# Folding the time steps of a chunked state-space scan into its decays' exponentials

## The chip, the cores and the metric

The kernel runs on one core of a Trainium2 chip. The core has a matrix engine (PE; its weight loads are shown apart as PEld), a vector engine (DVE), a scalar engine (ACT), GpSimd (POOL) and queues that issue transfers (SP's, ACT's and POOL's). Each engine works through its own instructions in the order in which they stand in the program and waits on semaphores for the others. The metric is the device time of one execution in microseconds. Three executions of the kernel before took 1017.43 to 1017.98 us, with a median of 1017.71.

## What is computed

One block of a hybrid network on 512 tokens of width 1024: an input projection, a convolution branch, a state-space branch (the "scan"), gates that mix the two, and a feed-forward part. The change lies in the scan. It has 32 heads of width 64 in 8 groups of 4; the part of the reference that matters, with `dt` the time steps after a softplus, is

```python
a_dt = dt * a                      # a = -exp(a_log)
a_cs = cumsum(a_dt)                # within a chunk
xdt = x * dt[..., None]
decay_in = exp(where(causal, a_cs[l] - a_cs[s], -inf))
y_diag = einsum("cls,rcls,csrp->clrp", C @ B.T, decay_in, xdt)
decay_to_end = exp(a_cs[-1] - a_cs)
chunk_states = einsum("cln,rcl,clrp->crpn", B, decay_to_end, xdt)
y = y_diag + y_off + x * d_skip
```

`y_off` carries the states from chunk to chunk. Afterwards y is gated by silu(z), normalised by group and projected.

## The kernel before

The scan is worked in 4 chunks of 128 tokens. For a group g, four steps are written as functions. `make_L(g)` fetches the running sums of the group's 4 heads to all partitions through a GpSimd transfer, masks them and forms the tile L by 16 Exp activations on ACT with the bias `nacs` (L496), the negated sums of the other token. `s1(g)` transposes the group's x from channel rows to token rows on PE (tiles pxT, two of 128x512 in PSUM, L667), multiplies each out of PSUM by the time steps (xdt, L670) and by D (y, L671) on DVE, multiplies xdt by the decay to the chunk's end (xdec, L675), transposes B (pBT), multiplies C and B (pcb) and multiplies L by that product (L686, 128x2048). `s2(g)` makes the chunk states (pSa, pSb from xdec and BT, L697), carries them on (prev, L698 to L701) and makes the diagonal part (yd from L and xdt, L709). `s3(g)` adds up y (L717, L734), multiplies by silu(z) and normalises; `s4(g)` transposes y (pyT, L761) and splits it into a high part and a rest (yh on ACT, yl on DVE) for the output projection.

Everything of one group runs beside the large projections of the next: `proj_x(g+1)`, then s1(g), `proj_bc(g+1,"B")` (tile pB), s2(g), `proj_bc(g+1,"C")` (pC), s3(g), and for odd g the gate projections pz (`proj_zz`). A projection is 24 matmuls of 128x512: three products (L246, L248, L252) of high parts (whi, hhi) and rests (wlo, hlo) for each of 8 blocks of 128. Each weight strip is cast to whi on ACT (L202); its rest wlo is made on DVE (L209) or by a GpSimd transfer onto a negated copy (L206, L207). After a projection `conv4` applies four taps: one on ACT out of PSUM (L599), three on DVE (L601), and a Silu on ACT (L605). DVE also works off the 31 taps of the other branch's convolution (tiles a, L514) wherever there is room.

The order on each engine is set by a scheduler that places the recorded instructions by their dependencies and its own estimates of their durations. `by_table` adds an edge that keeps the activations it is given (the Exps, the Silus) in the order of the program, so that the activation tables change seldom. PSUM tiles outside the projections take turns in three banks (`aux_tile`), so a tile can be written only after the tile three turns earlier was read. Before all that, `time_steps` and `running_sums` work out dt (tile dtt), the sums (acs), their exponentials (eacs, dec) and nacs for all heads at once, in tiles of 128x128.

Of the kernel before, what the change touches and what calls it, by code (L numbers as in the profile page):

```python
# [18 lines left out]
P = 128  # L19
# [145 lines left out]
def b3(ap, n):  # L165

    return ap.unsqueeze(len(ap.shape)).to_broadcast(list(ap.shape) + [n])
# [3 lines left out]
def block_kernel(ctx: ExitStack, tc: tile.TileContext, x, xT, x0, prm, hp, gp, wf, w, out):  # L171
# [149 lines left out]
    def flat(a):  # L321
        return a.rearrange("p a b -> p (a b)")
# [135 lines left out]
    def running_sums():  # L458
        pcs = aux_tile("pcs")
        pe.matmul(pcs[:, :CH], tri, flat(ta), start=True, stop=True)  # L460
        act.copy(flat(acs), pcs[:, :CH])
        pend = aux_tile("pend")
        pe.matmul(pend[:, :CH], ones, flat(ta), start=True, stop=True)
        act.activation(flat(cd), pend[:, :CH], AF.Exp)
        act.activation(flat(eacs), flat(acs), AF.Exp)
        dve.tensor_tensor(out=flat(tb), in0=pend[:, :CH], in1=flat(acs), op=ALU.subtract)
        act.activation(flat(dec), flat(tb), AF.Exp)
# [188 lines left out]
    def s1(g):  # L656
        s = st[g]
        hs = slice(HG * g, HG * (g + 1))
        xdt = ssd.tile([P, NT, HG, HD], F32, tag="xdt", name=f"xdt{g}")
        y = ssd.tile([P, NT, HG, HD], F32, tag="y", bufs=2, name=f"y{g}")  # L660
        xdec = ssd.tile([P, NT - 1, HG, HD], F32, tag="xdec", name=f"xdec{g}")
        for c2 in range(2):
            ps = aux_tile(f"pxT{g}_{c2}")
            for c in range(2):
                tok = slice((2 * c2 + c) * P, (2 * c2 + c + 1) * P)
                for e in range(2):
                    pe.transpose(ps[:, c * GW + e * P : c * GW + (e + 1) * P], s[f"x{e}"][:, tok], ident)  # L667
            cs = slice(2 * c2, 2 * c2 + 2)
            pv = ps.rearrange("p (c h d) -> p c h d", c=2, h=HG)
            dve.tensor_tensor(out=xdt[:, cs], in0=pv, in1=b3(dtt[:, cs, hs], HD), op=ALU.mult)  # L670
            dve.tensor_tensor(  # L671
                out=y[:, cs], in0=pv,
                in1=b3(hp_t[:, 2:3, hs].to_broadcast([P, 2, HG]), HD), op=ALU.mult,
            )
        dve.tensor_tensor(out=xdec, in0=xdt[:, : NT - 1], in1=b3(dec[:, : NT - 1, hs], HD), op=ALU.mult)  # L675
# [10 lines left out]
        dve.tensor_tensor(out=L, in0=L, in1=ps.unsqueeze(1).to_broadcast([P, HG, T]), op=ALU.mult)  # L686
        s.update(xdt=xdt, y=y, xdec=xdec, BT=BT)

    def s2(g):
        s = st[g]  # L690
        hs = slice(HG * g, HG * (g + 1))
        prev = ssd.tile([P, NT - 1, HG, HD], F32, tag="prev", name=f"prev{g}")
        tmp = ssd.tile([P, HG, HD], F32, tag="ptmp", bufs=2, name=f"ptmp{g}")
        pa, pb = aux_tile(f"pSa{g}"), aux_tile(f"pSb{g}")
        pS = [pa[:, :GW], pa[:, GW:], pb[:, :GW]]
        for c in range(NT - 1):
            pe.matmul(pS[c], s["BT"][:, c, :], s["xdec"][:, c].rearrange("p h d -> p (h d)"), start=True, stop=True)  # L697
        act.copy(prev[:, 0].rearrange("p h d -> p (h d)"), pS[0])  # L698
        for c in range(1, NT - 1):
            dve.tensor_tensor(out=tmp, in0=prev[:, c - 1], in1=b3(cd[:, c, hs], HD), op=ALU.mult)  # L700
            dve.tensor_tensor(  # L701
                out=prev[:, c], in0=pS[c].rearrange("p (h d) -> p h d", h=HG), in1=tmp, op=ALU.add
            )
        yd = [yd_tile(n, f"yd{g}_{n}").rearrange("p (c h d) -> p c h d", c=2, h=HG) for n in range(2)]
        for c in range(NT):
            for h in range(HG):
                for i in range(0, P, HD):
                    half = slice(i, i + HD)
                    pe.matmul(yd[c // 2][half, c % 2, h, :], s["L"][:, h, c, half], s["xdt"][:, c, h, :], start=True, stop=True)  # L709
        s.update(prev=prev, yd=yd)  # L710

    def s3(g):
# [1090 lines left out]
```

## Time and profile before

| | |
|---|---|
| three executions, median (lowest to highest) | 1017.71 us (1017.43 to 1017.98) |
| span of the profiled execution, first to last instruction | 1016.0 us |
| median less span | 1.7 us |
| instructions in the profiled execution | 15943 |
| busiest engine but PE | DVE, 847.9 us (83% of the span) |
| GpSimd busy | 106.7 us (11%) |
| granted PE clock, mean over the span | 0.998 of full speed |

The profiled execution's own time is not listed apart from its span; the row "median less span" is what lies around the span, by the three timed executions. The scan with its projections runs from about 110 us to 520 us of the span. A row of the timeline reads: start in us, duration in us, engine, line, operation, output and inputs, shape, and in brackets how long the engine sat idle before it and what ended that. Successive matmuls overlap in the record, so a matmul's place is read from the start of the next one.

### The profile page before, as it was taken

To read this page: it belongs to the slowest core of one execution; us is meant where nothing else is said; L and a number is where in the kernel's file an instruction comes from. 1 tells how busy PE (TensorE), PEld (TensorE's weight loads), DVE (VectorE), ACT (ScalarE), POOL (GpSimd) and SP (SyncE) were. 2 spreads that over 40 slices of the span, in tenths; PEclk is the share of its full clock that TensorE was granted. 3 is DMA by queue.
4 is the path that set the end of the run, shared out by engine and by line. 5 is a ranking of instruction groups with operands and counts; after the bars stand their busy time and mean duration, and the time that the engine had idled before them with its cause. 6 is when DMAs were issued, how large, how long until landed. Compare 5 with 4: busy or idle time off the path is not lost.

```text
span 1016.0 us, 15943 instructions
## 1 busy us (share of the span) xinstructions
PE 1007.7 (99%) x6184; PEld 881.7 (87%) x6184; DVE 847.9 (83%) x1233; ACT 616.9 (61%) x1038; POOL 106.7 (11%) x138
## 2 busy tenths in 40 slices
PE   9999999999999999999999999999999999999997
PEld 7898889888888888888888889889999999998886
DVE  7899977868696879678987889788999887899974
ACT  7655775667666746573552685466666566568552
POOL 0101202120121011100110111012000000001001
PEclk9999999999999999999999999999999999999999
DMA  8567635645554465356452355624755555469622
GB/s 302 151 168 218 158 96 145 187 110 144 158 151 117 130 182 151 102 135 163 99 139 69 114 142 165 223 104 118 230 151 160 153 143 146 128 177 295 212 83 83
DMA packets 43803, 155.02 MB, mean 153 GB/s; under 512 B 5072, under 2 KB 6096, under 8 KB 42704
## 3 DMA queue, kind: packets, MB, share of 16 engines
q1 hardware_dynamic: 30672, 105.44, 30.7%
q0 software_dynamic: 11136, 43.00, 21.7%
q10 hardware_dynamic: 1920, 5.57, 1.6%
q8 instruction: 48, 0.79, 0.3%
q14 instruction: 27, 0.22, 0.1%
HBM read 149.73 MB, written 4.26 MB: 152 GB/s over the span
## 4 chain that ended last, share of the span: by engine, by line
PE 87%; DVE 8%; ACT 3%; issue 1%; DMA 1%; SPq 0%; POOL 0%; POOLq 0%; DVEq 0%; ACTq 0%
PE xy L246 4%; PE xy L252 4%; PE xy L248 4%; PE pso L246 3%; PE pso L248 3%; PE pso L252 3%; PE yv L246 2%; PE yv L252 2%; PE yv L248 2%; PE px L246 2%; PE px L252 2%; PE px L248 2%; DVE a L514 2%; PE pz L248 2%; PE pz L252 2%; PE pz L246 2%
## 5 line engine op out<-in xcount | busy, mean ns | idle before, releaser
L514 DVE SCALAR_TENSOR_TENSOR a<-v,prm_t,a 128x511 f32<-128x511 f32 (+15 forms) x240 | 183.8, 769 | 14.3 <-ACT a L511 12.3
L202 ACT CAST whi<-raw 128x1024 fp32r<-128x1024 f32 x99 | 102.6, 1048 | 127.9 <-PE pso L248 36.7
L209 DVE TENSOR_TENSOR wlo<-raw,whi 128x1024 fp32r<-128x1024 f32 x58 | 70.6, 1220 | 32.7 <-ACT whi L202 32.5
L207 POOL DMA_DIRECT2D wlo<-in_w x41 | 36.5, 891 | 369.1 <-ACT wlo L206 171.4
L248 PE MATMUL pz<-wlo,hhi 128*128 128x512 f32 (+2 forms) x160 | 56.2, 351 | 0.2
L252 PE MATMUL pz<-whi,hlo 128*128 128x512 f32 (+2 forms) x160 | 56.1, 352 | 0.0
L246 PE MATMUL pz<-whi,hhi 128*128 128x512 f32 (+2 forms) x160 | 55.4, 353 | 0.0
L246 PE MATMUL px<-hhi,whi 128*128 128x512 f32 x128 | 50.2, 392 | 0.0
L246 PE MATMUL pso<-yh,whi 128*128 128x512 f32 x128 | 50.2, 394 | 0.0
L252 PE MATMUL px<-hhi,wlo 128*128 128x512 f32 x128 | 49.8, 389 | 0.0
L248 PE MATMUL px<-hlo,whi 128*128 128x512 f32 x128 | 49.8, 389 | 0.0
L248 PE MATMUL pso<-yl,whi 128*128 128x512 f32 x128 | 49.8, 390 | 0.0
L252 PE MATMUL pso<-yh,wlo 128*128 128x512 f32 x128 | 49.7, 390 | 0.0
L1189 ACT CAST whi_g<-raw 128x1024 fp32r<-128x1024 f32 x40 | 41.2, 1052 | 10.6 <-PE yv L248 4.9
L601 DVE SCALAR_TENSOR_TENSOR x<-px,prm_t,x 128x511 f32<-128x511 f32 (+2 forms) x48 | 34.7, 743 | 13.9 <-ACT x L599 13.8
L1196 DVE TENSOR_TENSOR wlo_g<-raw,whi_g 128x1024 fp32r<-128x1024 f32 x34 | 41.3, 1221 | 3.5 <-ACT whi_g L1189 3.4
L206 ACT ACTIVATE wlo<-whi 128x1024 fp32r<-128x1024 f32 x41 | 43.3, 1055 | 0.3
L496 ACT ACTIVATE L<-L,nacs 128x128 f32<-128x128 f32 x128 | 38.8, 389 | 0.1
L248 PEld LDWEIGHTS pz<-wlo,hhi 128*128 128x128 f32 x160 | 30.1, 188 | 4.9 <-DVE wlo L209 1.0
L246 PEld LDWEIGHTS pz<-whi,hhi 128*128 128x128 f32 x160 | 30.2, 189 | 3.9
L252 PEld LDWEIGHTS pz<-whi,hlo 128*128 128x128 f32 x160 | 30.1, 188 | 3.7
L1189 ACT CAST chi_g<-raw 128x1024 fp32r<-128x1024 f32 x24 | 24.9, 1053 | 8.8 <-PE yv L248 3.4
(763 smaller groups left out, 3450.7 us busy)
## 6 DMA issues: line engine op xcount, KB each, us to landing
raw<-in_w SPq DMA_DIRECT2D x182, 512.0 KB, 4.5
wlo<-in_w POOLq DMA_DIRECT2D x41, 512.0 KB, 6.8
L<-scr POOLq DMA_DIRECT2D x8, 1024.0 KB, 7.6
wlo_g<-in_w POOLq DMA_DIRECT2D x11, 512.0 KB, 7.0
clo_g<-in_w POOLq DMA_DIRECT2D x6, 512.0 KB, 5.5
pws<-in_w POOLq DMA_DIRECT2D x8, 256.0 KB, 5.9
pw_raws<-in_w SPq DMA_DIRECT2D x4, 512.0 KB, 7.0
xr<-in_x ACTq DMA_DIRECT2D x4, 512.0 KB, 3.9
```

Of the source, the lines that this page charges most:

```text
L202: mark[n, c.start] = act.copy(hi[:, c], src)
L206: act.activation(lo[:, c], hi[:, c].bitcast(F32), AF.Copy, scale=-1.0)
L207: mark["lo"] = pool.dma_start(lo[:, c], w[n][:, c].bitcast(F32R), accum_op=ALU.add)
L209: mark["wlo"] = dve.tensor_tensor(out=lo[:, c], in0=src, in1=hi[:, c].bitcast(F32), op=ALU.subtract)
L246: mark["pe"] = pe.matmul(ps, lh, rh, start=start, stop=False, skip_group_check=more)
L248: pe.matmul(ps, lh, rl, start=False, stop=False, skip_group_check=more)
L252: mark["pe3"] = pe.matmul(ps, ll, rh, start=False, stop=stop, skip_group_check=more)
L496: act.activation(L[:, h, c, :], L[:, h, c, :], AF.Exp, bias=nacs[:, c, HG * g + h : HG * g + h + 1])
L514: return dve.scalar_tensor_tensor(out=va[j][:, d:], in0=vs[j][:, : T - d], scalar=col("dw_w", j * KC + KC - 1 - d), in1=va[j][:, d:], op0= ...
L601: dve.scalar_tensor_tensor(out=a[:, d:], in0=ps[:, : T - d], scalar=col("ssm_w", i * KS + KS - 1 - d), in1=a[:, d:], op0=ALU.mult, op1=ALU ...
L1189: a_ = act.copy(hi, src)
L1196: d_ = dve.tensor_tensor(out=lo, in0=src, in1=hi.bitcast(F32), op=ALU.subtract)
```

## The change

Two identities are used. The factor dt on x is moved into the exponentials: exp(s) times dt is exp(s + ln dt). So the bias of the Exps that make L becomes ln dt minus the running sum, dec is multiplied by dt once for all heads, and x itself, without dt, is the operand of both products. In `running_sums` this adds a multiplication of dec by dt, a maximum of dt with 1e-38, a logarithm on ACT with its table load, and a subtraction in the place of a negation, all of 128x128. In `s1`, x is copied out of the two PSUM tiles by two ACT copies in the order of `by_table`; xdec and y read this copy in SBUF, and y is made by one instruction of 128x1024 where two of 128x512 were. The instruction counts by program go from 1235 to 1213 on DVE and from 1000 to 1018 on ACT; PE's stay the same.

```diff
-        dve.tensor_scalar(out=flat(nacs), in0=flat(acs), scalar1=-1.0, scalar2=None, op0=ALU.mult)
+        dve.tensor_tensor(out=flat(dec), in0=flat(dec), in1=flat(dtt), op=ALU.mult)
+        dve.tensor_scalar(out=flat(dtt), in0=flat(dtt), scalar1=1e-38, scalar2=None, op0=ALU.max)
+        act.activation(flat(dtt), flat(dtt), AF.Ln)
+        dve.tensor_tensor(out=flat(nacs), in0=flat(dtt), in1=flat(acs), op=ALU.subtract)
...
-        xdt = ssd.tile([P, NT, HG, HD], F32, tag="xdt", name=f"xdt{g}")
+        xt = ssd.tile([P, NT, HG, HD], F32, tag="xdt", name=f"xt{g}")
...
-            dve.tensor_tensor(out=xdt[:, cs], in0=pv, in1=b3(dtt[:, cs, hs], HD), op=ALU.mult)
-            dve.tensor_tensor(
-                out=y[:, cs], in0=pv,
-                in1=b3(hp_t[:, 2:3, hs].to_broadcast([P, 2, HG]), HD), op=ALU.mult,
-            )
-        dve.tensor_tensor(out=xdec, in0=xdt[:, : NT - 1], in1=b3(dec[:, : NT - 1, hs], HD), op=ALU.mult)
+            by_table(act.copy(xt[:, 2 * c2 : 2 * c2 + 2].rearrange("p c h d -> p (c h d)"), ps))
+        dve.tensor_tensor(out=xdec, in0=xt[:, : NT - 1], in1=b3(dec[:, : NT - 1, hs], HD), op=ALU.mult)
+        dve.tensor_tensor(out=y, in0=xt, in1=b3(hp_t[:, 2:3, hs].to_broadcast([P, NT, HG]), HD), op=ALU.mult)
...
-                    pe.matmul(yd[c // 2][half, c % 2, h, :], s["L"][:, h, c, half], s["xdt"][:, c, h, :], start=True, stop=True)
+                    pe.matmul(yd[c // 2][half, c % 2, h, :], s["L"][:, h, c, half], s["xt"][:, c, h, :], start=True, stop=True)
```

The scheduler then places other instructions differently too. Lines behind the first edit are numbered three higher in the changed kernel, those behind the edits of s1 two lower: L599, L601, L605 become L602, L604, L608; L686, L697, L709, L761 become L684, L695, L707, L759.

First place, PE in group 1, after pB of group 2 (its last row is the first here). Before, pyT of group 0 and the states (pSa, pSb) come early in pC, and yd five matmuls later:

```order
L252 MATMUL pB_1795<-hhi,wlo_1555 128x512
L761 MATMUL pyT_0_1880<-ident,y_1355 128x128 x4
L246 MATMUL pC_1898<-hhi,whi_1686 128x512
L697 MATMUL pSa_1834<-xdec_1760,BT_1780 128x256 x2
L697 MATMUL pSb_1835<-xdec_1760,BT_1780 128x256
L248 MATMUL pC_1898<-hlo,whi_1686 128x512
L252 MATMUL pC_1898<-hhi,wlo_1687 128x512
L246 MATMUL pC_1898<-hhi,whi_1686 128x512
L248 MATMUL pC_1898<-hlo,whi_1686 128x512
L252 MATMUL pC_1898<-hhi,wlo_1687 128x512
L709 MATMUL yd_0_1844<-xdt_1758,L_1256 64x64 x16
L709 MATMUL yd_1_1845<-xdt_1758,L_1256 64x64 x16
```

and in the changed kernel:

```order
L252 MATMUL pB_1796<-hhi,wlo_1557 128x512
L246 MATMUL pC_1899<-hhi,whi_1688 128x512
L248 MATMUL pC_1899<-hlo,whi_1688 128x512
L252 MATMUL pC_1899<-hhi,wlo_1689 128x512
L246 MATMUL pC_1899<-hhi,whi_1688 128x512
L707 MATMUL yd_0_1845<-xt_1760,L_1259 64x64 x16
L707 MATMUL yd_1_1846<-xt_1760,L_1259 64x64 x3
L695 MATMUL pSa_1835<-xdec_1762,BT_1781 128x256 x2
L695 MATMUL pSb_1836<-xdec_1762,BT_1781 128x256
L707 MATMUL yd_1_1846<-xt_1760,L_1259 64x64 x13
L759 MATMUL pyT_0_1881<-ident,y_1358 128x128 x4
```

yd has moved ahead of pSa, four matmuls behind pB, and the pieces stand in one block; pyT has moved behind them. Groups 3 and 5 change alike, with twelve matmuls of pC ahead of yd, and pSa behind 29 and 23 of yd's 32.

Second place, ACT in group 1 (a is a tap's first step of the other convolution, x_0 and x_1 the two strips of group 2's x, BT the copy of pBT). Before:

```order
L496 ACTIVATE L_1659<-L_1659,nacs 128x128 x15
L202 CAST whi_1686<-raw_1546 128x1024
L599 ACTIVATE x_0_1714<-px_0_1683,prm_t 128x512
L202 CAST whi_1723<-raw_1552 128x1024
L599 ACTIVATE x_1_1752<-px_1_1720,prm_t 128x512
L206 ACTIVATE wlo_1724<-whi_1723 128x1024
L680 COPY BT_1780<-pBT_1776 128x384
L511 ACTIVATE a_1789<-v_570,prm_t 128x512
L202 CAST whi_1798<-raw_1684 128x1024
L605 ACT_TABLE_LOAD
L605 ACTIVATE x_0_1714<-x_0_1714 128x512
L605 ACTIVATE x_1_1752<-x_1_1752 128x512
```

and in the changed kernel, from the same convolution step on:

```order
L602 ACTIVATE x_0_1716<-px_0_1685,prm_t 128x512
L202 CAST whi_1725<-raw_1554 128x1024
L514 ACTIVATE a_1790<-v_570,prm_t 128x512
L206 ACTIVATE wlo_1726<-whi_1725 128x1024
L602 ACTIVATE x_1_1754<-px_1_1722,prm_t 128x512
L678 COPY BT_1781<-pBT_1777 128x384
L202 CAST whi_1799<-raw_1686 128x1024
L608 ACT_TABLE_LOAD
L608 ACTIVATE x_0_1716<-x_0_1716 128x512
L202 CAST whi_1902<-raw_1723 128x1024
L608 ACTIVATE x_1_1754<-x_1_1754 128x512
L671 COPY xt_1760<-pxT_0_1763 128x512
```

The first step of strip 1's convolution has moved behind two other instructions, and the two copies of x of group 1 (the second follows the one shown) stand behind both Silus of group 2's x; the cast of whi_1686's strip has moved ahead of the Exps.

Third place, DVE in the same stretch. Before:

```order
L671 TENSOR_TENSOR y_1759<-pxT_0_1761,hp_t 128x512
L601 SCALAR_TENSOR_TENSOR x_1_1752<-px_1_1720,prm_t,x_1_1752 128x509
L670 TENSOR_TENSOR xdt_1758<-pxT_1_1768,dtt 128x512
L671 TENSOR_TENSOR y_1759<-pxT_1_1768,hp_t 128x512
L675 TENSOR_TENSOR xdec_1760<-xdt_1758,dec 128x768
L686 TENSOR_TENSOR L_1256<-L_1256,pcb_1782 128x2048
```

and in the changed kernel:

```order
L604 SCALAR_TENSOR_TENSOR x_0_1716<-px_0_1685,prm_t,x_0_1716 128x509
L604 SCALAR_TENSOR_TENSOR x_1_1754<-px_1_1722,prm_t,x_1_1754 128x511
L684 TENSOR_TENSOR L_1259<-L_1259,pcb_1783 128x2048
L604 SCALAR_TENSOR_TENSOR x_1_1754<-px_1_1722,prm_t,x_1_1754 128x510
L517 SCALAR_TENSOR_TENSOR a_1790<-v_570,prm_t,a_1790 128x510
L604 SCALAR_TENSOR_TENSOR x_1_1754<-px_1_1722,prm_t,x_1_1754 128x509
L517 SCALAR_TENSOR_TENSOR a_1790<-v_570,prm_t,a_1790 128x509
L209 TENSOR_TENSOR wlo_1800<-raw_1686,whi_1799 128x1024
L672 TENSOR_TENSOR xdec_1762<-xt_1760,dec 128x768
L673 TENSOR_TENSOR y_1761<-xt_1760,hp_t 128x1024
```

The multiplication of L, which does not need x, has moved ahead of the last taps of strip 1, and xdec and y behind them and behind a tap of the other convolution and a weight rest. In groups 3 and 5 xdec and y stand later still: in group 3 between the second and third tap of group 4's B, in group 5 behind a weight rest and ahead of B's first tap.

More of the change, by code (lines that the diff above doesn't have):

```diff
@@ L667, in s1 @@
                     pe.transpose(ps[:, c * GW + e * P : c * GW + (e + 1) * P], s[f"x{e}"][:, tok], ident)
[L668 to L671, printed above, removed]
-                out=y[:, cs], in0=pv,
-                in1=b3(hp_t[:, 2:3, hs].to_broadcast([P, 2, HG]), HD), op=ALU.mult,
-            )
-        dve.tensor_tensor(out=xdec, in0=xdt[:, : NT - 1], in1=b3(dec[:, : NT - 1, hs], HD), op=ALU.mult)
+            by_table(act.copy(xt[:, 2 * c2 : 2 * c2 + 2].rearrange("p c h d -> p (c h d)"), ps))
+        dve.tensor_tensor(out=xdec, in0=xt[:, : NT - 1], in1=b3(dec[:, : NT - 1, hs], HD), op=ALU.mult)
+        dve.tensor_tensor(out=y, in0=xt, in1=b3(hp_t[:, 2:3, hs].to_broadcast([P, NT, HG]), HD), op=ALU.mult)
         ps = yd_tile(0, f"pBT{g}")
@@ L686, in s1 @@
         dve.tensor_tensor(out=L, in0=L, in1=ps.unsqueeze(1).to_broadcast([P, HG, T]), op=ALU.mult)
-        s.update(xdt=xdt, y=y, xdec=xdec, BT=BT)
+        s.update(xt=xt, y=y, xdec=xdec, BT=BT)
     def s2(g):
```

## The prediction

> **What bounds the kernel.** I read the page's busy times and slices first, then what PE and its weight loads waited for, then the costs by line, then the timeline where the change acts.
>
> ```profile
> PE 1007.7 (99%) x6184; PEld 881.7 (87%) x6184; DVE 847.9 (83%) x1233; ACT 616.9 (61%) x1038; POOL 106.7 (11%) x138
> ...
> PEclk9999999999999999999999999999999999999999
> ...
> PE 87%; DVE 8%; ACT 3%; issue 1%; DMA 1%; SPq 0%; POOL 0%; POOLq 0%; DVEq 0%; ACTq 0%
> ```
>
> PE is busy for 99% of the span at full clock, and the chain that ended last is 87% PE. Busy PE is a modelled figure, so I also read what is left to gain from the waits of PE and of its weight loads:
>
> ```profile
> PE warm_ps L334 <- DVE woken L329: 1.0, 1, 1.0
> PE pxT L667 <- DVE yl L763: 0.4, 1, 0.4
> PE xy L246 <- DVE f L1396: 0.2, 1, 0.2
> PE pv L568 <- DVE elo L367: 0.2, 1, 0.2
> ...
> PEld yd L709 <- issue: 1.4, 4, 0.4
> PEld pz L248 <- DVE wlo L209: 1.0, 2, 0.6
> ...
> PEld pxT L667 <- DVE yl L763: 1.0, 2, 0.8
> ```
>
> That is the whole stock: 1.8 us of PE waits, 1.0 of it before the first projection, and some single microseconds of weight loads, which run ahead of their matmuls. Nothing that DVE or ACT is relieved of can give more than a part of this. So the question is not how much work the change takes from DVE, but where the new order makes PE wait.
>
> **What the change takes from DVE and gives to ACT.**
>
> ```profile
> L670 DVE TENSOR_TENSOR xdt<-pxT,dtt 128x512 f32<-128x512 f32 x16 | 10.9, 684 | 6.5 <-PE pxT L667 6.5
> L671 DVE TENSOR_TENSOR y<-pxT,hp_t 128x512 f32<-128x512 f32 x16 | 10.9, 682 | 0.0
> L675 DVE TENSOR_TENSOR xdec<-xdt,dec 128x768 f32<-128x768 f32 x8 | 7.6, 950 | 0.0
> L740 DVE TENSOR_TENSOR y<-y,z 128x1024 f32<-128x1024 f32 x5 | 6.1, 1214 | 0.0
> L780 ACT COPY so<-pso 128x512 f32<-128x512 f32 x8 | 4.6, 577 | 2.9 <-PE pso L252 2.9
> ```
>
> Per group four instructions of 0.68 us go (2.73 us) and one of 128x1024 comes. The trace has this shape with plain operands at 1.21 us; the 128x768 one with a broadcast operand, scaled by 4/3, gives 1.27. DVE saves about 1.5 us a group, 12 us in all. ACT gains two copies out of PSUM of 0.58 us, 9 us in all. DVE and ACT idle for 168 and 399 us of the span, so neither sum reaches the end of the program by itself: PE's matmuls cover both. If the cover were gone, as it would be behind a starved PE, the 12 us would be the prize.
>
> **The logarithm** stands in the last stretch before the scan, on ACT:
>
> ```profile
> 87.50 1.28 ACT L464 ACT_TABLE_LOAD   x1
> 88.79 0.28 ACT L464 ACTIVATE cd<-pend 128x128 f32<-128x128 f32 x1
> ...
> 90.27 0.30 ACT L467 ACTIVATE dec<-scratch 128x128 f32<-128x128 f32 x1
> ...
> 91.79 1.06 ACT L202 CAST whi<-raw 128x1024 fp32r<-128x1024 f32 x1 [1.22 <-PE pv L248]
> 97.23 1.06 ACT L202 CAST whi<-raw 128x1024 fp32r<-128x1024 f32 x1 [4.38 <-PE pg L248]
> ```
>
> Behind dec DVE has a multiplication, two taps and the maximum of 128x128; ACT has its four transfers to issue, then the load (1.28) and Ln (0.3 like Exp). So Ln ends near 93.3 and the first cast starts there in place of 91.79: 1.5 us late. Behind it ACT sat idle for 4.38 us, and strips are cast three ahead of their use (W_AHEAD in the code). Bounds are 0 and 1.6 us (load and Ln wholly exposed); I take 0. The Trainium skill ("ScalarE: Activation LUTs", What ACT_TABLE_LOAD costs) says a switch of tables costs a load of 1283 ns and a drain of 1380 ns. The load's row agrees; the next activation here starts as the load ends, so the drain isn't seen; with it Ln would end near 94.7, inside the same idle stretch, and the sum would be the same.
>
> **Where PE could now wait: group 1.** These rows of the timeline are ACT's, DVE's and PE's:
>
> ```profile
> 174.56 4.49 ACT L496 ACTIVATE L<-L,nacs 128x128 f32<-128x128 f32 x15
> 178.94 1.03 ACT L202 CAST whi<-raw 128x1024 fp32r<-128x1024 f32 x1
> 179.88 0.78 ACT L599 ACTIVATE x<-px,prm_t 128x512 f32<-128x512 f32 x1
> ...
> 183.47 0.82 ACT L511 ACTIVATE a<-v,prm_t 128x512 f32<-128x512 f32 x1
> ...
> 186.55 1.15 ACT L605 ACTIVATE x<-x 128x512 f32<-128x512 f32 x2
> ...
> 182.41 2.71 DVE L601 SCALAR_TENSOR_TENSOR x<-px,prm_t,x 128x510 f32<-128x510 f32 x4
> 188.34 2.28 DVE L686 TENSOR_TENSOR L<-L,pcb 128x2048 f32<-128x2048 f32 x1
> 191.84 1.22 DVE L209 TENSOR_TENSOR wlo<-raw,whi 128x1024 fp32r<-128x1024 f32 x1
> ...
> 188.62 0.60 PE L761 MATMUL pyT<-ident,y 128*128 128x128 f32 x4
> 191.04 0.40 PE L246 MATMUL pC<-hhi,whi 128*128 128x512 f32 x1
> 191.28 0.40 PE L248 MATMUL pC<-hlo,whi 128*128 128x512 f32 x1
> 191.83 2.08 PE L709 MATMUL yd<-xdt,L 128*64 128x64 f32 x64
> ```
>
> On ACT one cast moves ahead of the Exps, so strip 0's first convolution step starts at 179.9 as before. Then come a cast (0.95 from start to start), the a step (0.7), the lo copy (0.95), and only then strip 1's step, done by 183.9. On DVE strip 1's first tap follows (0.65), then L (2.2, to 186.8), then three taps (2.0, to 188.8). ACT's second Silu follows (0.55, to 189.5), then the copies: 190.1 and 190.6. PE leaves pB at 188.62, has four matmuls (0.23 each) and wants yd's operands at 189.5. It waits **0.6 us**, until 190.1. On DVE a tap and the lo rest (0.65 and 1.15) put xdec at 190.7 to 191.65, while PE has done 19 of 32 pieces of yd (1.2 us) by 191.3: **0.35 us** more. Together 0.95. What is queued behind PE here is all of pC; nothing but PE's own order waits for it. Ends: 0 if ACT runs 0.9 earlier; 2.2 if DVE loses 1.3 us in that stretch, as this tap did:
>
> ```profile
> 202.99 2.09 DVE L514 SCALAR_TENSOR_TENSOR a<-v,prm_t,a 128x504 f32<-128x504 f32 x1
> ```
>
> (the row's 2.09 less some 0.75 for a tap). I take 0.95, since the row lies 10 us behind the place.
>
> **Group 0** has copies behind Silus that DVE finishes in time; the same walk gives the copies' end at 149.1, where PE arrives with its third matmul of pC at 149.0: 0.
>
> **Groups 3 and 5.** Here the copies stand behind ACT's step for the next group's B and the Silu of its second x strip:
>
> ```profile
> 292.48 1.03 PE L697 MATMUL pSa<-xdec,BT 128*128 128x256 f32 x4
> ...
> 293.40 0.78 ACT L599 ACTIVATE B<-pB,prm_t 128x512 f32<-128x512 f32 x1
> ...
> 295.60 0.75 DVE L601 SCALAR_TENSOR_TENSOR B<-pB,prm_t,B 128x510 f32<-128x510 f32 x1
> ```
>
> In group 3 that step ends at 294.1, the Silu at 294.6, the copies at 295.2 and 295.7. PE has twelve matmuls from 292.48 and arrives at 295.2. xdec starts behind B's second tap, at 296.2, and ends at 297.2; PE has done 29 of 32 pieces (1.9 us) by 297.1. Both are level: I put 0.15 us. Group 5, a hundred microseconds on, has the same picture with wlo in place of the tap: 0.15 us. Ends for each: 0, and 0.95 as in group 1. Groups 2, 4 and 6 have two to four pieces of the output projection between the copies and pSa (some 5 us), group 7 a whole gate projection: 0.
>
> **What goes.** DVE, freed, makes its rests earlier: in groups 1 and 5 the two waits of pz for wlo (1.0 us of weight loads, less what the loads run ahead) should go: −0.75 us, between 0 and −1.0. The wait of pxT for yl is in group 2, with the same instructions before it on all engines: it stays.
>
> **Blocks on PE.** Turning from small matmuls back to a projection costs time:
>
> ```profile
> 303.20 0.59 PE L721 MATMUL pYb<-prev,C 128*128 128x256 f32 x2
> 303.44 0.58 PE L246 MATMUL pz<-whi,hhi 128*128 128x512 f32 x1
> 303.86 0.40 PE L248 MATMUL pz<-wlo,hhi 128*128 128x512 f32 x1
> ```
>
> The first matmul takes 0.42 from start to start, where 0.23 is usual: 0.19 a block. Counted from the order, 28 such blocks become 22: −1.1 us. But in groups 0, 1, 3 and 5 yd is cut by pSa. That turn isn't in the trace; its nearest row is this one, so 0 to 0.4 for going and coming: 0 to +1.6. From the middle, 0.25 each: +1.0. I take −0.1.
>
> **The sum.** 0.95 + 0.15 + 0.15 − 0.75 − 0.1 = +0.4 us on a span of 1016.0. The span plus 1.7 us around it is the median, 1017.7; the forecast is **1018.1 us**.
>
> **The rivals.** *Hidden after all* (0.22): ACT and DVE come ahead of my walk by a microsecond, no new wait arises, the two old ones go: −0.75 − 0.1, or 1016.9. For it speaks that DVE is rid of 2.7 us ahead of just these places; against it, that in group 1 the copies hang on ACT's order. *A wait in place of the multiplications, larger than I walk it* (0.15): the copies stand behind Silus that need DVE's last tap, and xdec behind more work of DVE than before. If DVE loses 1.0 to 1.3 us to something like the stretched tap in all of groups 1, 3 and 5, PE's waits are 2.2, 1.2 and 1.2 us: +4.6 − 0.85, or 1021.5; with two of the three, 1020.4. It decides at xdec's start, 296.2 in group 3: PE wants the result at 297.1, so each tenth later is a tenth of PE's. For it speaks that the scheduler placed these by its estimates, level with PE; against it, that DVE has lost 2.7 us of work ahead of xdec. *DVE was the hidden bound* (0.05): in groups 1, 3 and 5 it is hardly idle:
>
> ```profile
> 181.00:206.00 25.00, 25.00 (x180) 21.11 (x179) 24.31 (x35) 14.07 (x19) 4.38 (x4) 1.00 0.68 191
> ```
>
> DVE works 24.31 of 25 us there. If every wait listed for pz and pxT goes, the blocks give their 1.1 and nothing new arises, the gain is 1.0 + 1.0 + 1.1: 1014.6. Against it stands that PE too works all 25 of those 25 us.
>
> **Range and chances.** My forecast has 0.58, with its own range 1017.2 to 1019.5. The range takes in the hidden case's 1016.9, with the unknown turn's lower end (another −0.2), and the lighter half of the slow case: 1016.7 to 1020.4. Less than 0.2%, 2.0 us, can't be told from no change. Slower than 1019.75 is the slow case, 0.15; faster than 1015.67 the last one, 0.05; 0.80 lies between.
>
> **What would show it.** Right: PE's list of waits gains yd or its loads waiting for an ACT copy in group 1, for 0.5 to 1 us, and pSa waiting for xdec; pz no longer waits for wlo; DVE's busy time falls by about 12 us and ACT's rises by 9 to 11. Wrong: a wait of PE over 1 us in group 3 or 5; a cast behind Ln that PE waits for; pz waiting still.

## The result, and the profile after

The changed kernel takes 1020.41 us (median of 10 runs, 1019.89 to 1021.69); the kernel before, beside it, 1017.72 us (10 runs, 1016.89 to 1018.83). The ratio is 1.0028 with a 95% interval from 1.0019 to 1.0036: slower by 2.7 us, small but clear. The page of the changed kernel, its busy times, the granted clock and the chain:

```profile
PE 1009.1 (99%) x6184; PEld 882.0 (87%) x6184; DVE 836.6 (82%) x1211; ACT 626.3 (62%) x1056; POOL 108.6 (11%) x138
...
PEclk9999999999999999999999999999999999999999
...
PE 91%; DVE 3%; issue 2%; ACT 2%; DMA 1%; POOL 1%; SPq 0%; POOLq 0%; DVEq 0%; ACTq 0%
```

DVE has 11.3 us less to do and ACT 9.4 more, as forecast, and PE is as full as it was. What PE and its loads waited for:

```profile
PE warm_ps L334 <- DVE woken L329: 1.0, 1, 1.0
PE yd L707 <- ACT xt L671: 1.0, 1, 1.0
...
PEld yd L707 <- issue: 3.4, 10, 0.4
PEld yd L707 <- ACT xt L671: 2.5, 4, 1.5
...
PEld pxT L670 <- DVE yl L761: 0.4, 2, 0.2
PEld pz L248 <- DVE wlo L209: 0.4, 1, 0.4
```

One wait of 1.0 us is new, and the loads of yd stand at "issue" ten times in place of four: yd is begun more often (14 times in place of 9 by PE's rows). How much that costs the list doesn't say, so I compared PE's starts at the same matmul in both traces. The last px matmul of group 3 starts here before:

```profile
232.63 0.39 PE L252 MATMUL px<-hhi,wlo 128*128 128x512 f32 x1
```

and here after:

```profile
234.33 0.39 PE L252 MATMUL px<-hhi,wlo 128*128 128x512 f32 x1
```

1.70 us later; at the last px of group 2 it was 0.13 later (180.82 and 180.95). Between the two lies the scan of group 1, and it costs 1.57 us. So each group has its own number, and so has every experiment. All are against the one trace of before, in us, positive where PE has lost time; "6, 7" ends with the last pyT, "rest" with the program's last matmul. What comes ahead of the last px of group 1 differs by -0.9 to 0.0 from kernel to kernel, with no loss for those that have the logarithm, and is left out. Two kernels, e_g1dve and e_order, are missing: their profiled executions ran at a mean granted clock of 0.56 and 0.75 of full speed, so they have times alone.

| kernel | 0 | 1 | 2 | 3 | 4 | 5 | 6, 7 | rest | ratio to before, interval |
|---|---|---|---|---|---|---|---|---|---|
| the change | 0.45 | 1.57 | -0.58 | 0.41 | -0.05 | -0.01 | 0.57 | 0.24 | 1.0028 [1.0019, 1.0036] |
| e_cut | 0.45 | 0.97 | 0.80 | 0.47 | 0.38 | -0.01 | 0.93 | 0.64 | 1.0041 [1.0027, 1.0055] |
| e_head | 0.00 | 0.31 | 0.07 | 0.21 | 0.03 | -0.45 | 0.00 | 0.16 | 1.0005 [0.9996, 1.0014] |
| e_nobt | 0.01 | 1.28 | -0.56 | 0.03 | -0.01 | 0.04 | 0.59 | 0.34 | 1.0018 [1.0009, 1.0027] |
| e_uncut | 0.02 | 4.43 | -0.59 | 0.07 | -0.02 | -0.33 | 0.52 | 0.16 | 1.0041 [1.0029, 1.0054] |
| e_defer | 0.01 | 1.55 | -0.55 | 0.03 | -0.05 | -0.42 | 0.59 | -0.03 | 1.0017 [1.0008, 1.0026] |
| e_best | 0.01 | 1.63 | -0.58 | 0.00 | -0.05 | -0.35 | 2.49 | 0.19 | 1.0039 [1.0026, 1.0051] |
| e_dvecopy | 0.44 | 0.34 | -0.44 | 1.59 | 0.07 | -0.47 | 0.69 | 0.00 | 1.0020 [1.0011, 1.0028] |
| e_ypsum | -0.02 | 1.15 | -0.57 | 0.28 | 0.05 | -0.44 | 1.03 | 0.16 | 1.0019 [1.0010, 1.0028] |
| e_mix1 | 0.01 | 1.23 | -0.55 | 0.00 | -0.04 | -0.43 | 0.55 | 0.11 | 1.0011 [1.0002, 1.0020] |
| e_mix16 | 0.01 | 1.33 | -0.55 | 0.00 | -0.02 | -0.29 | 1.31 | 0.35 | 1.0023 [1.0013, 1.0032] |
| e_order_nobt | 0.01 | 2.33 | -0.59 | 0.00 | -0.04 | -0.35 | 0.51 | 0.17 | 1.0013 [1.0004, 1.0022] |
| e_taps | 0.01 | 3.76 | -0.57 | 0.00 | -0.04 | -0.45 | 0.55 | 0.11 | 1.0033 [1.0020, 1.0045] |
| e_few | 0.01 | 1.24 | -0.53 | 0.62 | -0.04 | -0.44 | 0.13 | 0.44 | 1.0016 [1.0006, 1.0025] |
| e_few_before | 0.00 | 0.34 | -0.51 | 0.11 | 0.12 | 1.75 | -0.75 | 0.28 | 1.0010 [1.0001, 1.0020] |
| e_g0dve | 0.01 | -0.36 | -0.53 | 0.00 | -0.04 | -0.43 | 0.56 | 0.17 | 0.9996 [0.9988, 1.0005] |
| e_g06dve | 0.01 | -0.38 | -0.55 | 0.00 | -0.02 | -0.45 | 1.28 | 0.09 | 1.0003 [0.9994, 1.0012] |

The change's row adds up to 2.6 us; with the -0.3 ahead of it that is the 2.3 by which the two profiled spans differ (1018.3 and 1016.0), and the medians differ by 2.7. Most of it stands in groups 0, 1, 3 and 6. In e_few_before the columns 5 and "6, 7" go together, +1.0 us: transposes and products of group 6, about 1.2 us of work, stand ahead of the last px of group 7 there, and behind it in all the others. Group 1 in the changed kernel, on PE, ACT and DVE (start, duration, engine and line):

```profile
189.43 0.39 PE L246 MATMUL pC<-hhi,whi 128*128 128x512 f32 x1
190.85 0.57 PE L707 MATMUL yd<-xt,L 128*64 128x64 f32 x12 [1.03 <-ACT xt L671]
...
192.33 1.13 PE L695 MATMUL pSa<-xdec,BT 128*128 128x256 f32 x4
...
192.33 0.73 PEld L695 LDWEIGHTS pSa<-xdec,BT 128*128 128x128 f32 x4 [0.24 <-DVE xdec L672]
...
172.92 1.71 ACT L746 ACTIVATE y<-y,rs 128x256 f32<-128x256 f32 x4 [1.85 <-POOL rs L259]
...
180.62 0.76 ACT L602 ACTIVATE x<-px,prm_t 128x512 f32<-128x512 f32 x1
...
182.22 0.81 ACT L514 ACTIVATE a<-v,prm_t 128x512 f32<-128x512 f32 x1
182.94 1.05 ACT L206 ACTIVATE wlo<-whi 128x1024 fp32r<-128x1024 f32 x1
183.89 0.76 ACT L602 ACTIVATE x<-px,prm_t 128x512 f32<-128x512 f32 x1
...
189.69 0.63 ACT L608 ACTIVATE x<-x 128x512 f32<-128x512 f32 x1 [0.84 <-DVE x L604]
190.23 1.05 ACT L671 COPY xt<-pxT 128x512 f32<-128x512 f32 x2
...
181.42 0.75 DVE L604 SCALAR_TENSOR_TENSOR x<-px,prm_t,x 128x511 f32<-128x511 f32 x1 [8.69 <-ACT x L602]
...
185.35 2.28 DVE L684 TENSOR_TENSOR L<-L,pcb 128x2048 f32<-128x2048 f32 x1
187.54 0.74 DVE L604 SCALAR_TENSOR_TENSOR x<-px,prm_t,x 128x510 f32<-128x510 f32 x1
188.20 0.74 DVE L517 SCALAR_TENSOR_TENSOR a<-v,prm_t,a 128x510 f32<-128x510 f32 x1
188.86 0.74 DVE L604 SCALAR_TENSOR_TENSOR x<-px,prm_t,x 128x509 f32<-128x509 f32 x1
```

ACT waits 0.84 us for strip 1's last tap, the copies follow the Silu at 190.23, and yd starts a microsecond after PE is free for it. The tap of 188.20 belongs to the other convolution, and nothing in these rows waits for it. The lateness starts further ahead: strip 0's first step is 0.74 us later than before (180.62 and 179.88), since ACT had sat idle for 1.85 us until GpSimd had made rs, a factor of the normalisation, and the table load and all 16 Exps stand behind that; before, the load and one Exp stand ahead of it (171.35 and 172.65). DVE waited for that step, 8.69 us.

### The profile page after: what moved, and what is told of

The parts are those of the page before. It is cut to its first block, busy times and chain, and to the rows that moved or that the text cites. A ratio compares the mean times of both kernels' runs of the same rounds, so it can differ in the third digit from the quotient of the medians.

```text
span 1018.3 us, 15949 instructions
## 1 busy us (share of the span) xinstructions
PE 1009.1 (99%) x6184; PEld 882.0 (87%) x6184; DVE 836.6 (82%) x1211; ACT 626.3 (62%) x1056; POOL 108.6 (11%) x138
## 4 chain that ended last, share of the span: by engine, by line
PE 91%; DVE 3%; issue 2%; ACT 2%; DMA 1%; POOL 1%; SPq 0%; POOLq 0%; DVEq 0%; ACTq 0%
PE xy L246 4%; PE xy L252 4%; PE xy L248 4%; PE pz L248 3%; PE pso L246 3%; PE pz L246 3%; PE pz L252 3%; PE pso L248 3%; PE pso L252 3%; PE px L246 2%; PE px L248 2%; PE px L252 2%; PE yv L248 2%; PE yv L246 2%; PE yv L252 2%
## 5 line engine op out<-in xcount | busy, mean ns | idle before, releaser
L517 DVE SCALAR_TENSOR_TENSOR a<-v,prm_t,a 128x511 f32<-128x511 f32 (+15 forms) x240 | 180.2, 754 | 16.5 <-ACT a L514 14.0
L604 DVE SCALAR_TENSOR_TENSOR x<-px,prm_t,x 128x511 f32<-128x511 f32 (+2 forms) x48 | 34.9, 742 | 27.9 <-ACT x L602 27.8
```

What stands on the lines that cost most here:

```text
L517: return dve.scalar_tensor_tensor(out=va[j][:, d:], in0=vs[j][:, : T - d], scalar=col("dw_w", j * KC + KC - 1 - d), in1=va[j][:, d:], op0= ...
L604: dve.scalar_tensor_tensor(out=a[:, d:], in0=ps[:, : T - d], scalar=col("ssm_w", i * KS + KS - 1 - d), in1=a[:, d:], op0=ALU.mult, op1=ALU ...
```

## The experiments

The edits are shown shortened, with some names spelled out. `not_before(a, b)` makes the scheduler place a behind b; pS stands for pSa and pSb, and a copy is "tied" when it is given to `by_table`.

**The cut alone (e_cut).** The kernel before, with pS in the middle of yd:

```diff
+ last_s = pe.matmul(pS[c], ...)
+ not_before(last_s, pieces[18])        # yd's 19th matmul
+ for m in pieces[19:]: not_before(m, last_s)
```

> The kernel before, with nothing of the change but the cut: in every group pS (three 128x256 matmuls) stands behind the 19th of yd's 32 pairs of half-blocks' matmuls and the rest of yd behind pS. Theory 'turns on PE': going from yd to pS and back costs about 0.4 us a cut, read on PE's starts in groups 3 and 5, where nothing else moves; groups 0 and 1 give one turn back to a projection less (0.2 each): +2.5 to +3 us for the eight cuts, ratio 1.0025 to 1.003. Rival 'waits only' (the cut is free and the change's +2.7 us are operands that come late): within 0.3 us of before, ratio 1.000, and no excess in groups 3 and 5.

Group 3 of e_cut, where nothing else moved:

```profile
294.40 0.39 PE L252 MATMUL pB<-hhi,wlo 128*128 128x512 f32 x1
294.72 1.38 PE L702 MATMUL yd<-xdt,L 128*64 128x64 f32 x38
296.03 1.13 PE L705 MATMUL pSa<-xdec,BT 128*128 128x256 f32 x4
297.00 0.59 PE L705 MATMUL pSb<-xdec,BT 128*128 128x256 f32 x2
297.52 1.03 PE L702 MATMUL yd<-xdt,L 128*64 128x64 f32 x26
298.48 0.66 PE L766 MATMUL pyT<-ident,y 128*128 128x128 f32 x4
```

and of the kernel before:

```profile
292.25 0.40 PE L252 MATMUL pB<-hhi,wlo 128*128 128x512 f32 x1
292.48 1.03 PE L697 MATMUL pSa<-xdec,BT 128*128 128x256 f32 x4
293.35 0.59 PE L697 MATMUL pSb<-xdec,BT 128*128 128x256 f32 x2
293.87 2.08 PE L709 MATMUL yd<-xdt,L 128*64 128x64 f32 x64
295.89 0.65 PE L761 MATMUL pyT<-ident,y 128*128 128x128 f32 x4
```

From pB's last matmul to pyT: 4.08 us with the cut, 3.64 without. The same 64 and 6 passes take **0.44 us** longer with no wait in between, and group 5 loses the same 0.44 up to its pyT. From start to start, 0.25 of it lies in the two pieces of yd (1.31 and 0.96, where 2.02 was whole), 0.10 in the pSa behind the first piece, and 0.09 in the last matmul of pB, now followed by yd. "Turns on PE" holds for the cut. It doesn't hold for the turn back to a projection: group 0 has one less in e_cut and still loses 0.45. In the whole, +4.1 us is more than forecast, since yd was also broken by the output projection in group 2 (0.80) and the waits of pz for wlo in group 1 grew.

**The logarithm alone (e_head).** The kernel before, with the floor, Ln and the subtraction, their result unused:

> The kernel before, with the floor of the steps, the load of the logarithm's table, Ln and the subtraction added in the running sums, their result unused. Theory of the prediction: hidden, within 0.3 us of before (ratio 1.000). Rival 'logarithm': the first casts of the scan come 1.5 us later and PE loses 1 to 1.6 us there, ratio 1.001 to 1.0016.

1.0005, no difference that can be told. But the logarithm isn't in the change's place here: nothing ties it to dec, and it ran at 82.09, where the change has it at 92.61. That it is hidden there too is read from the changed kernel itself: its PE, at the same matmuls, is 0.29 us ahead of before at 88 us and 0.32 ahead at 98 us, so nothing is lost in between. This run has before's order on PE behind the head, so it also shows what a group's number is worth: group 1 has +0.31 and group 5 -0.45, both through waits of pz for wlo that came and went by themselves.

**The copies untied (e_nobt), and yd not cut with the copies tied (e_uncut).**

```diff
-            by_table(act.copy(xt[...], ps))
+            act.copy(xt[...], ps)            # e_nobt
...
+ not_before(yd_matmul, last_s)              # e_uncut, tie kept
```

> The changed kernel, where the copies of x out of PSUM are no longer tied to the order of ACT's table users, so that they stand ahead of the Silus and pS ahead of yd; logarithm, copies on ACT and D x in one step stay. Theory 'order of the copies' (the tie makes the copies late, and that gives both the wait of group 1 and the cuts): 2.2 to 2.9 us less than the changed kernel, within 0.5 us of before (ratio 0.9995 to 1.0005), no wait of yd for an ACT copy. Rival 'the work itself' (the logarithm, ACT's added copies or the one step of 1024 cost): stays at +2 us or more over before, ratio 1.002 to 1.003. Rival 'turns on PE only': the cuts' 1.6 us go, the wait of 1.2 us stays: +1.

> The changed kernel with the tie of the copies kept, and yd's matmuls not before the last of pS. Theory 'turns on PE': the four cuts' 0.4 us each go, and PE fills the place with the projection of C: +0.6 to +1.2 us over before (ratio 1.0006 to 1.0012). Rival 'waits only': pS needs xdec, which needs both copies; PE waits for it instead, so +2 to +3 us stay (ratio 1.002 to 1.003), with pSa waiting for xdec in the list of PE's waits for 0.5 us a group.

Untied, the kernel takes 1019.08 us, 1.6 over before: groups 0, 3 and 5 cost nothing any more (no cut there), but group 1 keeps 1.28. That is the third theory's picture ("the wait stays"), though its time was +1, and it is another wait:

```profile
PE pSa L695 <- DVE xdec L672: 0.8, 1, 0.8
```

In e_uncut (1021.71 us, 4.2 over before, more than either theory has) groups 0, 3 and 5 are free too, with the tie kept: so the 0.4 of these groups is the cut and not the late copies. Group 1 got worse by a wait that neither theory had: pyT needs the bank of PSUM that the tied copy frees.

```profile
PE pyT L759 <- ACT xt L671: 2.6, 1, 2.6
```

**Copies by DVE (e_dvecopy), D x out of PSUM in two steps (e_ypsum).**

```diff
-            by_table(act.copy(xt[...], ps))
+            dve.tensor_copy(out=xt[...], in_=ps)                       # e_dvecopy
...
+            dve.tensor_tensor(out=y[:, cs], in0=ps, in1=D, op=mult)    # e_ypsum, in place of one step from xt
```

> The changed kernel with x copied out of PSUM by DVE in place of ACT; logarithm and D x in one step stay. Only group 0 has yd cut by pS now, and group 6 has it whole. Theory 'ACT's queue and turns': no wait of yd for x in group 1, one cut of 0.4 us: 0 to +0.8 us over before (ratio 1.000 to 1.0008). Rival 'the one copy ahead of both products': DVE's chain copy, copy, xdec is as long as before's, and stands behind the same taps: PE waits for xdec or L in group 1 as in the untied kernel, +1.2 to +2.

> The changed kernel with D x in two steps of 512 out of PSUM, as before the change; logarithm and the tied copies on ACT stay. yd stands whole ahead of pS in groups 0, 1, 3 and 5 (there pS cuts transposes or the projection), and is cut in groups 4, 6 and 7. Theory 'ACT's queue and turns': group 1 keeps its wait of yd for the copy (1.2 us), groups 0, 3 and 5 cost 0.2 or less each, 4, 6 and 7 up to 0.4: +1.5 to +2.2 over before. Rival 'the step of 1024 elements': DVE's later D x is what delays PE, so the loss goes: within 0.4 of before.

With DVE's copies group 1 costs 0.34, no more than in e_head. But group 3 now loses 1.59, where pYa, the part of y that comes from the states, waits 1.4 us for prev on DVE, and the whole is +2.3 us: neither theory's sum. In e_ypsum yd waits 1.5 us for the tied copy, as "ACT's queue and turns" has it, and the sum fits (+1.9); D x in one step is not the cause.

**Three repairs (e_defer, e_best, and copies of group 1 on DVE).** e_defer unties the copies and, in group 1, moves them ahead of the next strips' Silus and xdec ahead of L; e_best adds yd of group 6 behind the output projection's pieces, and in the other groups yd behind pS:

```diff
+ not_before(silu_of_group_2, copy_of_group_1)
+ not_before(L_times_CB, xdec); not_before(D_x, L_times_CB)    # group 1 alone
+ not_before(yd_matmul, mark["pe3"])                           # e_best, group 6
```

> The changed kernel with the copies untied, and in group 1 put where their operands are there: both copies ahead of the Silus of the next group's x strips on ACT, and the decay's product xdec ahead of the product L times CB, D x behind it, on DVE. Theory 'late operands in group 1' (the wait of 1.0 us of the untied kernel is xdec behind L, since the second copy comes late): the 1.3 us that group 1 costs there go, to 0.3 or less, and the whole is 0 to 0.6 us over before (ratio 0.9998 to 1.0008). Rival 'ACT has too much to do in that stretch' (16 us of 25 with the copies): the wait moves to another operand of PE (L, or the strip's Silu), and group 1 still costs over 0.8.

> As the run before, and in group 6 yd behind the output projection's pieces 2 and 3, in place of being cut by them. Theory 'turns on PE': group 6 gives back the 0.4 us that it costs in the changed kernel; the whole is within 0.5 us of before, rather below it than above, since the shorter wait of pxT for yl in group 2 (0.5 us) stays (ratio 0.9993 to 1.0003). Rival 'the cut of group 6 costs nothing by itself, it is a late L': the 0.4 us stay.

xdec is there when PE comes, and the wait has moved on, in e_defer's list:

```profile
PE pyT L771 <- DVE prev L711: 1.8, 1, 1.8
```

Group 1 costs 1.55. In e_best the mended group 6 pays with pso, the output projection, waiting 0.6 for a tap of B, and pSb 0.8 for yl: 2.49 for groups 6 and 7 in place of e_defer's 0.59, and 3.7 us over before. Then group 1's copies went to DVE, with the rest tied (e_g1dve), with the rest untied (e_mix1), and group 6's too (e_mix16):

```diff
+            if g in (1,):        # (1, 6) in e_mix16
+                dve.tensor_copy(out=xt[...], in_=ps)
+            else: act.copy(xt[...], ps)      # by_table(...) in e_g1dve
```

> The changed kernel with group 1's two copies alone on DVE; all others on ACT and tied to the table's order as in the change. Theory 'ACT's queue in group 1' (the copies stand on ACT behind convolution steps, casts and a table load, and whatever hangs on them comes late): group 1 falls from 1.6 us to 0.4 or less and the rest stays, so +0.9 to +1.3 us over before (ratio 1.0009 to 1.0013). Rival 'group 1 is full on all engines' (shifting the copy to DVE only makes xdec, L or prev late instead): group 1 still costs 1.1 us or more, +2 in all.

> The changed kernel, copies untied, group 1's on DVE. Theory 'ACT's queue in group 1, and turns on PE': no cut in groups 0, 1, 3 and 5, no wait in group 1; what is left is the cut of yd by the output projection in group 6 and the turns of group 7 (0.6 us together), less the 0.55 of group 2: 0 to +0.4 us over before (ratio 1.0000 to 1.0005). Rival 'group 1 is full on all engines': +1.2 to +1.5, like the untied kernel with ACT's copies.

> As the run before, and group 6's copies on DVE too, which leaves yd whole there. Theory 'turns on PE': 0.4 us less than with group 1's alone, read on PE's starts between the last px of group 7 and the last pyT: -0.4 to +0.1 us against before (ratio 0.9996 to 1.0002). Rival 'the cut of group 6 is free': no difference to the run before.

e_g1dve: 1019.83 us, 1.0026 [1.0015, 1.0036], +2.5 us and so the rival's time. e_mix1: group 1 costs 1.23 with the copies on DVE, with this wait:

```profile
PE yd L710 <- DVE L L687: 1.6, 1, 1.6
```

So the engine of the copy isn't the cause: L is late in place of x, as the rival has it, whose +1.2 to +1.5 the whole just misses (+1.0). In e_mix16 yd is whole in group 6, but a wait of pSb for yl in group 7 (0.9) takes the cut's place: 1.31 for the two groups, 0.55 in e_mix1, and +2.5 us in all, more than either expectation has.

**PE's order mended (e_order, e_order_nobt), the other convolution's taps put back (e_taps), fewer of them (e_few, e_few_before).** pS of group 1 behind part of the projection of C, then yd, then the rest, then pyT; in e_taps the taps of the loop's third pass behind prev; in e_few fewer of them:

```diff
+ if g == 2: proj(pC, w, ks=slice(0, 3))      # 6 in e_order, which keeps the tie
+ not_before(last_s, last_of_these)           # group 1
+ not_before(tap, last_prev)                  # e_taps
-TAPS = (6, 14, 18, 20, 20, 20, 20, 20)
+TAPS = (6, 14, 8, 20, 20, 22, 24, 24)        # e_few, e_few_before
```

> The whole change as it is (logarithm, copies on ACT tied to the table's order, D x in one step), and only PE's order mended: yd not before the last of pS in every group, and in group 1 pS behind 18 of the 24 matmuls of the projection of C, pyT of group 0 behind all of them. Theory 'PE's order': the operands come late in group 1 whatever engine copies x, and that costs only because PE has been given pS or yd too early, with the rest of the projection queued behind; group 1 costs 0.4 us or less, groups 0, 3 and 5 nothing, and the whole is 0 to +0.7 us over before (ratio 1.0000 to 1.0007). Rival 'group 1 is full on DVE': the wait moves on to pyT, pYa or pz, and group 1 still costs 1.1 us or more.

> As the run before, but the copies untied, and pS of group 1 behind 9 matmuls of the projection of C. Theory 'PE's order': xdec is there when PE comes (in the untied kernel it came 1.0 us late, and nine matmuls are 2.0 us), so group 1 costs 0.4 us or less, and the whole is -0.3 to +0.5 us against before (ratio 0.9997 to 1.0005). Rival 'group 1 is full on DVE': the wait moves on to pyT or pYa, which need the next states, and group 1 still costs 1.1 us or more.

> As the run before (copies untied, PE's order mended), and the taps of the gate branch's convolution that filled DVE and ACT in group 1 put behind the next states prev of group 1. Theory 'taps ahead of what PE waits for' (before the change, D x and the multiplications by the steps stood there; the freed time went to taps that nothing waits for, ahead of the x strips' taps, xdec and prev): group 1 costs 0.5 us or less, with no wait of pYa, pYb or pyT, and the whole is -0.6 to +0.5 us against before (ratio 0.9994 to 1.0005). Rival 'group 1 is full on DVE whatever stands first': a wait of over 0.8 us for some operand remains in group 1.

> The run with the copies untied and PE's order mended (group 1 cost 2.3 us there), with ten of the 18 taps of the gate branch's convolution that are planned into the loop's third pass, the one that holds group 1, moved to the sixth to eighth (8, 22, 24 and 24 in place of 18, 20, 20 and 20). Theory 'group 1 is full on DVE' (24 us of 25 in the kernel before): with 6.5 us of taps less in it, nothing that PE wants is late, and group 1 costs 0.4 us or less; the later passes may cost more, since their DVE gets fuller. Rival 'it is the order, not the amount': some operand is late again, and group 1 costs over 1 us.

> The kernel before, with the same table of taps: what the table does without the change. Theory 'group 1 is full on DVE': before loses only its 0.3 us of waits of pz in group 1, so it gains at most 0.3 there, and it loses in groups 4 to 7 what yd's cut by the output projection (group 6) costs, 0.4: within 0.6 us of before.

e_order: 1019.02 us, 1.0014 [1.0005, 1.0023], 1.7 us over before, which is more than "PE's order" allows. e_order_nobt lost more in group 1 than before the repair, in three smaller waits:

```profile
PE pz L248 <- DVE wlo L209: 1.0, 1, 1.0
PE pYb L731 <- DVE yl L775: 0.5, 1, 0.5
PE pYa L731 <- DVE prev L711: 0.3, 1, 0.3
```

In e_taps (+3.3 us in all) one wait of 2.2 us came in their place, and in e_few, with ten taps less, one of 1.3, both of pYb for yl: the bank that pyT leaves. The theory "taps ahead" fell; its rival asked for a wait of over 0.8. "Full on DVE" asked for 0.4 or less in e_few; less work brought group 1 from 2.33 to 1.24, which is its rival's figure (over 1). In group 6, e_few has yd whole behind the output projection, and there the cut's 0.4 are back (0.13 for groups 6 and 7 in place of e_order_nobt's 0.51). Its control e_few_before gains the same 0.5 in group 2 without the change, but loses 1.0 in groups 5 to 7 together; at 1.0010 it is 0.8 us over before, a little more than expected.

**The order around group 1 (e_g0dve, e_g06dve).** One thing had been left: e_dvecopy was the only kernel with the whole change and without the loss, and on ACT it had strip 1's convolution step where the kernel before has it. Moving group 0's copies alone to DVE gives that order, while group 1's copies stay on ACT:

```diff
+            if g == 0:           # (0, 6) in e_g06dve
+                dve.tensor_copy(out=xt[...], in_=ps)
+            else: act.copy(xt[...], ps)
+ not_before(yd_matmul, last_s)
```

> The changed kernel, copies untied, group 0's two copies alone on DVE, yd not before the last of pS. Group 1 keeps its copies on ACT and D x in one step, but the scheduler now lays its place as in the kernel before: on ACT the second x strip's convolution step directly behind one cast, ahead of the other convolution's step and the lo copy; on PE pyT and a matmul of C ahead of yd. Theory 'the order laid around group 1' (neither the copies' engine nor the amount of work): group 1 costs 0.4 us or less, all else as in the untied kernel, so 0 to +0.5 us over before (ratio 1.0000 to 1.0005). Rival 'group 1 is full with the copies on ACT': 1.1 us or more there again, +1.3 or more in all.

> As the run before, with group 6's copies on DVE too, so that yd is whole in group 6 and pS7's second tile stands ahead of yd in group 7. Theory 'turns on PE': 0.4 us less than the run before, level with the kernel before or below it by up to 0.4 (ratio 0.9996 to 1.0001). Rival 'what is gained in group 6 comes back as a wait of pSb in group 7' (as it did, 1.0 us, with the copies of groups 1 and 6 on DVE): +0.5 over the run before.

e_g0dve takes 1017.00 us (11 runs) against 1017.50: 0.9996, not to be told from before. Group 1 has -0.36, about the wait of pz for wlo that also came and went in e_head. ACT in e_g0dve's group 1:

```profile
180.43 0.78 ACT L602 ACTIVATE x<-px,prm_t 128x512 f32<-128x512 f32 x1
181.10 1.03 ACT L202 CAST whi<-raw 128x1024 fp32r<-128x1024 f32 x1
182.03 0.78 ACT L602 ACTIVATE x<-px,prm_t 128x512 f32<-128x512 f32 x1
182.71 1.05 ACT L206 ACTIVATE wlo<-whi 128x1024 fp32r<-128x1024 f32 x1
183.66 1.05 ACT L674 COPY xt<-pxT 128x512 f32<-128x512 f32 x2
```

Strip 1's step stands at 182.03 in place of 183.89, the copies at 183.66 in place of 190.23. The stretch from 181 to 206 us by engines (length, then PE, PEld, DVE, ACT, POOL busy), after:

```profile
181.00:206.00 25.00, 23.87 (x173) 19.87 (x172) 24.49 (x34) 15.87 (x22) 4.36 (x4) 1.00 0.64 170
```

and in e_g0dve:

```profile
181.00:206.00 25.00, 25.00 (x180) 21.11 (x179) 24.93 (x37) 17.06 (x24) 4.37 (x4) 1.00 0.67 191
```

DVE and ACT do more there than in the changed kernel, and PE doesn't wait at all. e_nobt has the same copies on ACT in group 1, and pS whole ahead of yd too, and loses 1.28. So group 1's loss is neither the copies nor the amount of work, but which instructions stand ahead of those that PE wants. Strip 1's step marks it: it starts 0.7 to 1.2 us behind the last px matmul of group 2 in all seven traces where none of yd, pS, pY and pyT waits in group 1 (before, e_cut, e_head, e_dvecopy, e_few_before, e_g0dve, e_g06dve), and 2.9 to 5.6 us behind it in the eleven others, which lose 1.15 or more there. No run moved this step alone, so that it is the cause by itself isn't shown. e_g06dve (1017.52 us, 1.0003) shows group 6's loss coming back in group 7 once more (1.28), as its rival has it.

## Why the prediction was wrong

- **PE as the bound, the work moved:** right. DVE's busy time fell by 11.3 us (12 forecast), ACT's rose by 9.4 (9 to 11), and none of it reached the end.
- **The logarithm at 0:** right, by PE's starts in the changed kernel. The first cast behind Ln starts at 92.83 after, 1.0 us later than before, and PE doesn't notice.
- **Group 1, 0.95:** the place and the operand were right, and the waits come to about that: yd waits 1.03 for the copy, and pSa's weight load 0.24 for xdec, some 0.1 of it at the matmul. Yet the terms were 0.6 and 0.35, so that the sum is near is luck. The walk went wrong at its first step, "strip 0's first convolution step starts at 179.9 as before": it starts at 180.62, behind ACT's wait for rs. All that follows is as much late: L ends at 187.5 for 186.8, strip 1's last tap at 189.6 for 188.8, and the copies start at 190.2 for 189.5. The rest of group 1's 1.57 is the cut's 0.45.
- **Groups 3 and 5, 0.15 each for a wait:** no wait came. They lose 0.41 and 0.44 by the cut. Group 5's row shows -0.01 only because a wait of pz went that goes in e_head too.
- **"Blocks on PE", -0.1, is the step that failed, in both of its terms.** A cut costs 0.44 (e_cut), outside the 0 to 0.4 that I gave it and not the 0.25 that I took: 1.8 in the four groups. And the six fewer turns, which are there (28 before and 22 after, by PE's rows too), give nothing, for the 0.19 a turn was misread. In a block the passes of 128x256 start 0.22 us apart (pSa's four above run from 292.48 to 293.35). In the rows that I priced, pYb's two passes and pz's first matmul run from 303.20 to 303.86, which is 0.66; two passes of 0.22 and a matmul of 0.23 are 0.67. So the turn costs nothing: the next matmul only starts early, and its 0.42 hold the rest of the small pass. The untied kernel has a turn less in group 0 and gains nothing (0.01). So where -0.1 stood, the runs show 1.8, and 2.2 with group 6's cut: nearly all of the 2.3 us by which the sum was short.
- **Groups 2, 4, 6, 7 at 0:** wrong for group 6. I counted yd's cuts by pSa and overlooked that the output projection cuts it there (21 matmuls, 24 of pso, then 11): 0.57 for groups 6 and 7, of which e_few shows 0.4 to be this cut. The kernel before cuts pYa there, which costs nothing that shows.
- **The old waits, -0.75 from pz in groups 1 and 5:** group 1's stayed. Group 5's went, but goes without the change as well. The wait of pxT for yl in group 2, which "stays", shrank: -0.58, as it also does in e_few_before, when only the table of taps moves.
- **The rivals:** the time came out where "a wait larger than I walk it" has it, 1020.4 to 1021.5, but through one wait of 1.0 and five cuts, not through three waits, so that this rival's number fits is luck. *Hidden after all* needed what e_g0dve has: 1017.00 us.

What stays open: which of the scheduler's estimates turns group 1's order when the copies of group 0 change engines, and which of the instructions that change places there would be enough alone. The orders were read, the estimates were not.

## What to carry to other kernels

Where one engine is 99% busy and runs in order, price a change by the new order on that engine: count every place where a block of small matmuls is cut, check that the price of a turn isn't a matmul that only started early, measure one cut in a kernel that is otherwise unchanged, and compare the engine's starts at the same instructions before and after, stage by stage. A wait that is mended by hand at one operand moves on to the next one (xt, xdec, L, prev, yl and wlo here, in ten experiments) as long as the order ahead of them stays; look for what is late first, here a convolution step on ACT by all that the traces show, before forbidding orders. And a loss after moving work between engines needn't be the moved work: here it went away with seven of eight groups' copies still moved.

## What the runs showed of the hardware

In two traces PE ran at half speed behind a wait. In e_uncut the matmuls behind the wait of 2.6 us start 0.43 us apart in place of 0.23, and the granted clock (last but two in the row) falls:

```profile
185.00:189.40 4.40, 4.40 (x21) 3.66 (x20) 4.40 (x6) 4.37 (x7) 0.93 (x1) 1.00 0.80 178
192.40:195.90 3.50, 3.46 (x11) 2.98 (x12) 3.43 (x5) 3.12 (x4) 0.88 (x1) 0.52 0.67 213
```

So with a wait of 2.6 us group 1 cost 4.4. It was the same in e_taps (2.2 us, then 0.60 for 4 us), but not behind the waits of 1.9 in e_best and 1.8 in e_defer. The Trainium skill ("TensorE: Matmul & The Clock Gate", What's actually happening) has the clock halved after an idle window of about 3.4 us; here less was enough.

A tap on DVE that should take 0.75 us took 2.09 at 202.99 in the kernel before, the row from which I priced a DVE loss. GpSimd's mask of L stands beside it:

```profile
202.53 2.01 POOL L489 TENSOR_SCALAR_AFFINE_SELECT L<-L 128x2048 f32<-128x2048 f32 x1 [7.63 <-DMA L<-scr]
```

The tap, both of whose tensors lie in SBUF, ends 0.5 us behind the mask. So do all seven taps that begin beside a mask in this trace; they take 1.66 to 2.40 us. In e_nobt the mask met instructions that read PSUM, and they kept their time:

```profile
203.13 2.01 POOL L492 TENSOR_SCALAR_AFFINE_SELECT L<-L 128x2048 f32<-128x2048 f32 x1 [7.91 <-DMA L<-scr]
...
203.54 0.68 DVE L715 TENSOR_TENSOR y<-yd,y 128x512 f32<-128x512 f32 x1
204.14 0.74 DVE L604 SCALAR_TENSOR_TENSOR C<-pC,prm_t,C 128x509 f32<-128x509 f32 x1
```

The Trainium skill ("SBUF — State Buffer", SBUF: two separate sides) says that a DVE instruction with two SBUF inputs and a GpSimd one that reads SBUF lock each other out for their whole length; these rows agree. So the price of 1.3 us for each of groups 1, 3 and 5 in the slow rival hung on whether a tap meets that mask, and group by group it needn't.
